# Partition sums of the modulation and gates of a decoder block: reductions with a 32x32 transpose on VectorE in the place of products with ones on TensorE

## The chip, the cores and the metric

The kernel is one program on one core of a Trainium2 chip. The metric is the device time of one execution in microseconds (us); the time of a kernel is the median of its runs. Five engines matter here: TensorE (PE in the profile, with its weight loads as PEld), VectorE (DVE), ScalarE (ACT), GpSimd (POOL) and SyncE (SP, which here only issues transfers).

## The reference: what is computed

One decoder block for 512 tokens of 1024 features in float32. Only the lines around the change are shown.

```python
cs = jax.nn.silu(c)                                   # (1, 1024)
mod = cs @ ada_w[l] + ada_b[l]                        # (1, 6 * 1024)
sh_m, sc_m, gt_m, sh_f, sc_f, gt_f = jnp.split(mod, N_MOD, axis=-1)
h = modulate(rmsnorm(x, norm_mix_g[l]), sh_m, sc_m)   # h * (1 + scale) + shift
...
merged = jax.nn.sigmoid(g_a) * y_a + jax.nn.sigmoid(g_b) * y_b
x = x + gt_m[:, None, :] * (merged @ mix_w_out[l])
h = modulate(rmsnorm(x, norm_ffn_g[l]), sh_f, sc_f)
f = (jax.nn.silu(h @ ffn_w_gate[l]) * (h @ ffn_w_up[l])) @ ffn_w_down[l]
x = x + gt_f[:, None, :] * f
return rmsnorm(x, final_norm_g)
```

The six vectors of `mod` are each a product of a 1024-vector with a 1024x1024 matrix. `sh_f` and `sc_f` (the feed-forward's modulation) and `gt_m` and `gt_f` (the two gates) are what the change touches.

## The kernel before

**The large products.** Every weight matrix is split into a high and a low part (`w_..._h` by a cast on ACT, `w_..._l` by a subtraction on DVE), and a product is three matmuls: low times high, high times low, high times high. One product of 128 output features for 512 tokens is 8 x 3 = 24 matmuls of 512 columns. Such a product is named after its output: `p_ga`, `p_gb` (merge gates), `p_ya`, `p_yb` (output projections of the two mixers), `mix`, `p_fg`, `p_fu` (feed-forward gate and up), `dn_b`, `dn_t` (blocks of the down projection). Each loop goes over pairs of 128 features: in the stage of `ga` and `ya`, an iteration is two products `p_ga` and two `p_ya`; in the next stage two `p_gb` and two `p_yb`.

**The vectors of mod.** A column of `mod` is a sum over 1024 rows of `ada_w`, laid out as 8 rows in each of 128 partitions. `ada_sum` adds the 8 rows of a partition on DVE, each scaled by its element of `cs`, into `acc_f` (512 columns: 256 of the shift and 256 of the scale) or `acc_gt_m`, `acc_gt_f` (256 columns). What is then left is the sum over the 128 partitions:

- For the modulation, `mod_vecs` has four matmuls for each of the four pairs of blocks, with 128 columns of `acc_f` as the weights and one column of ones as the moving side. The sums stand in `mod_f`, one feature in each partition, and `mod_cols` makes the columns `a_f` and `s_f` of them, which the second norm uses.
- For a gate, `gate_vec` splits each `acc` into `gh` and `gl`, multiplies both by a 128x128 tile of ones (`onesr`), so that every partition of `gp_gt_m` or `gp_gt_f` holds the sum, and adds it to `gt_m` or `gt_f`, into which the bias had been loaded, spread over all partitions. `add_gated` (for `gt_m`) and `add_gated_sum` (for `gt_f`) multiply by them.

**The order of the work.** The program is written in stages, and the framework's scheduler places each instruction in its engine's queue; every engine works its queue in order. `tick()` is called after each product, and `after(n, fn)` puts work behind the n-th tick from there: the four `summed(j)` of a gate came at ticks 1, 3, 5 and 7, each `spread(j)` one tick later. Loads of weights and of `ada_w` go through three buffers (`raw`) in the order of SP's queue. `block_sums` writes weights back to DRAM through POOL's queue (`blocks`). Early in the program, DVE works on `rotary_steps` (the angles) between the first products; the lines recorded there as L62 and L64 are those of a helper.

Of the kernel before, what the change touches and what calls it, by code (L numbers as in the profile page):

```python
# [11 lines left out]
F32 = mybir.dt.float32  # L12
F32R = mybir.dt.float32r
# [3 lines left out]
ALU = mybir.AluOpType  # L17
AX = mybir.AxisListType

P = 128  # L20
S = 512
D = 1024
H = 8
KT = D // P
# [9 lines left out]
ADA = {n: i * D for i, n in enumerate(("sh_m", "sc_m", "gt_m", "sh_f", "sc_f", "gt_f"))}  # L34
# [36 lines left out]
def block_kernel(ctx, tc, x, c, positions, ada_w, ada_b, norm_mix_g, w_in, conv_w, ret_w_out,  # L71
                 conv_w_out, mix_w_out, norm_ffn_g, ffn_w_gate, ffn_w_up, ffn_w_down,
                 final_norm_g, inv_freq, decay, out):
    nc = tc.nc
    pe, vec, act, pool, sync = (InTurn(tc, e) for e in (nc.tensor, nc.vector, nc.scalar, nc.gpsimd,
                                                        nc.sync))
    mm, transpose = pe.matmul, pe.transpose

    cp = ctx.enter_context(tc.tile_pool(name="cp", bufs=1))
# [3 lines left out]
    sp = ctx.enter_context(tc.tile_pool(name="sp", bufs=4))  # L83
    ps = ctx.enter_context(tc.tile_pool(name="ps", bufs=4, space=bass.MemoryType.PSUM))
    dp = ctx.enter_context(tc.tile_pool(name="dp", bufs=1, space=bass.MemoryType.DRAM))

    def slot(name, dt=F32, shape=None):
        return tp.tile(shape or [P, S], dt, tag="slot", name=name)

    def scr(name, dt=F32, shape=None):  # L90
        return tp.tile(shape or [P, S], dt, tag="scr", bufs=12, name=name)
# [7 lines left out]
    def aux(name, shape=None):  # L99
        return ps.tile(shape or [P, S], F32, tag="aux", bufs=2, name=name)  # L100
# [18 lines left out]
    def split_act(src, name, hi=None, lo=None, eng=None):  # L119
        hi = slot(name + "_h", F32R) if hi is None else hi  # L120
        lo = slot(name + "_l", F32R) if lo is None else lo
        act.copy(hi, src)
        (eng or vec).tensor_tensor(lo, src, hi.bitcast(F32), ALU.subtract)
        return hi, lo
# [12 lines left out]
    R_ADA, R_GM, R_GF, R_CW = 0, 48, 56, 64  # L137
# [4 lines left out]
    ident = cp.tile([P, P], F32, name="ident")  # L142
    make_identity(nc, ident)
    ones32 = cp.tile([P, P], F32, name="ones32")
# [27 lines left out]
    onesr = cp.tile([P, P], F32R, name="onesr")  # L172

    vecs = []
# [10 lines left out]
    def ada_sum(pieces, n, name, a=None, k0=0):  # L185

        first = a is None
        if first:
            a = sp.tile([P, n], F32, tag="adaacc", bufs=2, name=f"acc_{name}")
        for k, w in enumerate(pieces, k0):  # L190
            if first and k == k0:
                vec.tensor_scalar_mul(a, w, cs[:, k:k + 1])
            else:
                vec.scalar_tensor_tensor(a, w, cs[:, k:k + 1], a, ALU.mult, ALU.add)
        return a

    mod = {}
# [4 lines left out]
    ada_raw = {}  # L202
    def ada_load(f, j):


        s0 = 0 if f == "m" else 3
        cols = slice(j * P, (j + 2) * P)
        ada_raw[f, j] = pieces = []
        for k in range(0, KT, 4):
            raw = wp.tile([P, 4, 2, 2 * P], F32, tag="raw", bufs=3, name=f"ada_{f}{j}_{k}")  # L210
            for q, i in ((q, i) for q in range(0, 4, 2) for i in range(2)):
                load_raw.last = sync.dma_start(raw[:, q:q + 2, i],
                                               aw6[:, k + q:k + q + 2, s0 + i, cols])
            pieces += [raw[:, q].rearrange("p s n -> p (s n)") for q in range(4)]

    def mod_scale(f, k, col):
        g = (R_GM if f == "m" else R_GF) + k
        vec.scalar_tensor_tensor(mod["a_" + f][:, k:k + 1], col, vecs[0][:, g:g + 1],
                                 mod["b_" + f][:, k:k + 1], ALU.mult, ALU.add)

    def mod_shift(f, k, cols, n):
        r = R_ADA + ADA["sh_" + f] // P + k
        vec.tensor_tensor(mod["s_" + f][:, k:k + n], cols, vecs[0][:, r:r + n], ALU.add)

    def mod_cols(f, j, pt):

        mod_scale(f, j, pt[:, 2:3])
        mod_shift(f, j, pt[:, 0:2], 2)
        mod_scale(f, j + 1, pt[:, 3:4])

    def mod_gains(f):

        r0 = R_ADA + ADA["sc_" + f] // P
        g0 = R_GM if f == "m" else R_GF
        vec.scalar_tensor_tensor(mod["b_" + f], vecs[0][:, r0:r0 + KT], 1.0, vecs[0][:, g0:g0 + KT],
                                 ALU.add, ALU.mult)

    def mod_vecs(f, j):

        pt = aux(f"mod_{f}{j}")  # L240
        a = ada_sum(ada_raw.pop((f, j)), 4 * P, f"{f}{j}")
        for i in range(4):
            mm(pt[:, i:i + 1], lhsT=a[:, i * P:(i + 1) * P], rhs=ones32[:, 0:1],
               start=True, stop=True)
        mod_cols(f, j, pt)


    def half_ss(part, s, h, name):
# [147 lines left out]
    a = ada_sum(ada_raw["m", 0][2:6], 4 * P, "m0", None, 2)  # L396
# [155 lines left out]
    def after(n, fn):  # L552
        later.append([n, fn])
# [90 lines left out]
    def proj(src, col, Ah, Al, name, eng=None):  # L644
        raw = load_raw(src, 0, KT, col, 2 * P, "w_" + name)
        for i in range(2):
            wh, wl = split(raw[:, :, i * P:(i + 1) * P], [P, KT, P], f"w_{name}{i}", eng)
            yield i, fm_gemm(acc(f"p_{name}{i}"), wh, wl, Ah, Al)
            tick()
# [137 lines left out]
    def ret_out(p):  # L787
        raw = wp.tile([P, KT, 2 * P], F32, tag="raw", bufs=3, name=f"w_ya{p}")
        src = ret_w_out[0, :, 2 * p * P:2 * (p + 1) * P].rearrange(
            "(q h e c) n -> h e c q n", h=2, e=2, c=64)  # L790
        dst = raw.rearrange("p (q e) n -> p e q n", e=2)
        for h in range(2):
            for e in range(2):
                load_raw.last = nc.sync.dma_start(dst[64 * h:64 * h + 64, e], src[h, e])
        for i in range(2):
            wh, wl = split(raw[:, :, i * P:(i + 1) * P], [P, KT, P], f"w_ya{p}{i}")
            yield i, fm_gemm(acc(f"p_ya{p}{i}"), wh, wl, ret_in, None)
            tick()

    m_a = [None] * KT  # L800
    with tc.issue_after(hlast[-1].ins):
        mod_gains("f")
    merged = [None] * KT
    for p in range(KT // 2):
        sg = {}
        for i, pt in proj(wi, COL["ga"] + 2 * p * P, Hh, Hl, f"ga{p}"):
            sg[i] = scr(f"sga{p}{i}")
            act.activation(sg[i], pt, AF.Sigmoid)
        for i, pt in ret_out(p):
            vec.tensor_tensor(sg[i], pt, sg[i], ALU.mult)  # L810
            m_a[2 * p + i] = sg[i]
        ada_load("f", 2 * p)
        mod_vecs("f", 2 * p)
        if p == 0:
            next(block_steps)
    gate = {}

    def gate_vec(name):
        gate[name] = [misc(f"{name}_{h}") for h in range(2)]
        for h in range(2):  # L820
            with tc.issue_after(load_raw.last.ins):
                nc.sync.dma_start(
                    gate[name][h],
                    ada_b[0, ADA[name] + h * S:ADA[name] + (h + 1) * S].partition_broadcast(P))
        parts = {}

        def summed(j):
            raw = wp.tile([P, KT, 2 * P], F32, tag="raw", bufs=3, name=f"ada_{name}{j}")
            col = ADA[name] + 2 * j * P
            load_raw.last = nc.sync.dma_start(raw, aw[:, :, col:col + 2 * P])  # L830
            a = ada_sum([raw[:, k] for k in range(KT)], 2 * P, f"{name}{j}")
            gh = sp.tile([P, 2 * P], F32R, tag="gh", bufs=1, name=f"gh_{name}{j}")
            gl = sp.tile([P, 2 * P], F32R, tag="gl", bufs=1, name=f"gl_{name}{j}")
            parts[j] = split_act(a, "", gh, gl)

        def spread(j):
            gh, gl = parts.pop(j)
            pt = aux(f"gp_{name}{j}")
            mm(pt[:, 0:2 * P], lhsT=onesr, rhs=gl, start=True, stop=False)
            mm(pt[:, 0:2 * P], lhsT=onesr, rhs=gh, start=False, stop=True)  # L840
            gv = gate[name][j // 2][:, (j % 2) * 2 * P:(j % 2 + 1) * 2 * P]
            vec.tensor_tensor(gv, gv, pt[:, 0:2 * P], ALU.add)

        for j in range(4):
            after(2 * j + 1, lambda j=j: summed(j))
            after(2 * j + 2, lambda j=j: spread(j))

    for p in range(KT // 2):
        sg = {}
# [3 lines left out]
        for i, pt in proj(conv_w_out[0], 2 * p * P, conv_in, None, f"yb{p}"):  # L853
            f = 2 * p + i
# [98 lines left out]
    for i in range(2):  # L953
        wh, wl = [], []
        for k in range(0, KT, 4):
            h, l = split_act(raw[:, k:k + 4, i * P:(i + 1) * P], "",
                             slot(f"w_fg0{i}_{k}h", F32R, [P, 4, P]),
                             slot(f"w_fg0{i}_{k}l", F32R, [P, 4, P]))
# [196 lines left out]
    for h in range(2):  # L1155
# [15 lines left out]
        for t, cs in tm_gemm(ffn_w_down[0], af, f0, nf, h, groups, nf - 6, "dn", True):  # L1171
# [10 lines left out]
            r = sp.tile([P, 1], F32, tag="rr", name=f"nf_{t}_r")  # L1182
            i = 1 + cs.start // HS
            act.activation(r, ss3[t][:, i:i + 1], AF.Sqrt, scale=1.0 / D, bias=ss3[t][:, 0:1])
            vec.reciprocal(r, r)
            for i in (1, 0):
                o = scr(f"o_{t}{i}")
# [40 lines left out]
```

## Time and profile before

| | us |
|---|---|
| median of 3 runs | 947.89 |
| lowest and highest of them | 947.38, 948.22 |
| the profiled execution: its own time | 947.26 |
| its span, first to last instruction | 945.2 |
| PE busy in the span | 936.5 |
| DVE busy | 634.4 |
| ACT busy | 363.2 |
| POOL busy | 9.5 |

The span is 2.1 us shorter than the execution's time: that is what lies around the instructions. A row of the timeline has the start and the length of an instruction (or of several alike, with their count), the engine, the line, the operation, output and inputs by their names in the program, and the shapes. Matmuls overlap: each of 512 columns is shown as 0.39 us long, and the next starts about 0.23 us after it. So a matmul's price is the distance between starts, not its length.

### The profile page before, as it was taken

The numbers are of one execution on the slowest core, as the hardware profiler recorded it, in microseconds if no ns is written. First come the engines' busy times: TensorE is split into PE (matmuls) and PEld (weight loads), VectorE is DVE, ScalarE is ACT, GpSimd is POOL, SyncE is SP. The second block draws the span as 40 slices with busy tenths as digits, with TensorE's granted clock in tenths as the row PEclk, the third lists the DMA queues.
The fourth block names the chain that finished last, engine by engine and source line by source line (L and its number), as shares of the span: only waits on it lengthen the run. The fifth ranks groups of instructions, "written<-read, shape, count | busy, mean of one in ns | idle before, by whom it ended". The sixth has DMA issues, their size and how long they took to land.

```text
span 945.2 us, 11083 instructions
## 1 busy us (share of the span) xinstructions
PE 936.5 (99%) x4367; PEld 783.7 (83%) x4367; DVE 634.4 (67%) x981; ACT 363.2 (38%) x537; POOL 9.5 (1%) x26
## 2 busy tenths in 40 slices
PE   9999999999999999999999999999999999999997
PEld 8888888888888888888888888988888888888886
DVE  5989784898778755654664457657787535883346
ACT  7535333554453423222223335524433234433224
POOL 2000000000000000000000000000000000000000
PEclk9999999999999999999999999999999999999999
DMA  9943412321642447776463541455666752553102
GB/s 311 348 151 112 155 52 94 101 94 53 227 139 89 142 134 240 198 205 218 130 196 120 165 150 42 135 161 172 211 190 209 243 172 89 178 179 112 67 22 89
DMA packets 113619, 144.02 MB, mean 152 GB/s; under 512 B 4180, under 2 KB 93312, under 8 KB 112544
## 3 DMA queue, kind: packets, MB, share of 16 engines
q1 hardware_dynamic: 112048, 134.50, 44.7%
q0 software_dynamic: 1376, 8.57, 2.4%
q8 instruction: 34, 0.56, 0.3%
q10 hardware_dynamic: 144, 0.26, 0.1%
q14 instruction: 17, 0.14, 0.0%
HBM read 132.83 MB, written 10.49 MB: 152 GB/s over the span
## 4 chain that ended last, share of the span: by engine, by line
PE 98%; DVE 0%; ACT 0%; issue 0%; POOL 0%; ACTq 0%; POOLq 0%
PE p_fu L64 13%; PE p_fg L64 12%; PE p_ga L64 5%; PE p_g L64 5%; PE p_gb L64 5%; PE p_v L64 5%; PE p_yb L64 5%; PE dn_t L64 5%; PE p_ya L64 5%; PE p_q L64 5%; PE p_k L64 4%; PE p_b L64 3%; PE p_u L64 3%; PE p_c L64 3%; PE dn_b L64 3%; PE dn L64 3%
## 5 line engine op out<-in xcount | busy, mean ns | idle before, releaser
L64 PE MATMUL p_fu<-Gh,w_fu_l 128*128 128x512 f32 x160 | 62.3, 389 | 0.0
L64 PE MATMUL p_fu<-Gh,w_fu_h 128*128 128x512 f32 x160 | 62.3, 389 | 0.0
L64 PE MATMUL p_fg<-Gh,w_fg_l 128*128 128x512 f32 x160 | 62.3, 389 | 0.0
L64 PE MATMUL p_fg<-Gh,w_fg_h 128*128 128x512 f32 x160 | 62.2, 389 | 0.0
L64 PE MATMUL p_fu<-Gl,w_fu_h 128*128 128x512 f32 x160 | 62.2, 389 | 0.0
L64 PE MATMUL p_fg<-Gl,w_fg_h 128*128 128x512 f32 x160 | 62.2, 389 | 0.0
L64 DVE TENSOR_TENSOR w_fg_l<-w_fg,w_fg_h 128x1024 fp32r<-128x1024 f32 x20 | 24.4, 1222 | 36.7 <-ACT w_fg_h L64 36.7
L64 ACT CAST w_fu_h<-w_fu 128x1024 fp32r<-128x1024 f32 x20 | 21.1, 1054 | 60.5 <-PE p_fu L64 34.2
L64 ACT ACTIVATE fg<-p_fg 128x512 f32<-128x512 f32 x22 | 13.2, 598 | 73.8 <-PE p_fg L64 73.6
L64 DVE TENSOR_TENSOR fg<-p_fu,fg 128x512 f32<-128x512 f32 x22 | 15.2, 690 | 36.2 <-PE p_fu L64 36.2
L64 DVE TENSOR_TENSOR w_b_l<-w_b,w_b_h 128x1024 fp32r<-128x1024 f32 x18 | 22.0, 1221 | 19.8 <-ACT w_b_h L64 19.8
L64 PEld LDWEIGHTS p_fg<-Gh,w_fg_l 128*128 128x128 f32 x160 | 30.0, 188 | 6.2
L64 PEld LDWEIGHTS p_fg<-Gl,w_fg_h 128*128 128x128 f32 x160 | 30.0, 188 | 6.2
L64 PEld LDWEIGHTS p_fu<-Gh,w_fu_h 128*128 128x128 f32 x160 | 30.0, 188 | 6.2
L64 PEld LDWEIGHTS p_fu<-Gl,w_fu_h 128*128 128x128 f32 x160 | 30.0, 188 | 6.2
L64 PEld LDWEIGHTS p_fu<-Gh,w_fu_l 128*128 128x128 f32 x160 | 30.0, 188 | 6.2
L64 PEld LDWEIGHTS p_fg<-Gh,w_fg_h 128*128 128x128 f32 x160 | 30.0, 188 | 6.2
L64 DVE TENSOR_TENSOR w_bl<-w_bl 128x512 f32<-128x512 f32 x32 | 22.0, 689 | 7.5 <-DMA w_bl<-in_ffn_w_down_dram 7.1
L64 DVE TENSOR_TENSOR w_fu_l<-w_fu,w_fu_h 128x1024 fp32r<-128x1024 f32 x20 | 24.4, 1220 | 3.9 <-ACT w_fu_h L64 3.9
L64 ACT CAST sh<-sm 128x512 fp32r<-128x512 f32 (+3 forms) x32 | 14.7, 458 | 31.7 <-DVE sm L64 31.7
L64 DVE SCALAR_TENSOR_TENSOR acc_f<-ada_f,cs,acc_f 128x512 f32<-128x512 f32 x28 | 21.0, 750 | 8.7 <-DMA ada_f<-in_ada_w_dram 7.8
L64 ACT CAST w_b_h<-w_b 128x1024 fp32r<-128x1024 f32 x18 | 18.9, 1051 | 18.6 <-PE p_fu L64 8.0
(420 smaller groups left out, 2731.4 us busy)
## 6 DMA issues: line engine op xcount, KB each, us to landing
w_fg<-in_ffn_w_gate_dram SPq DMA_DIRECT2D x11, 1024.0 KB, 5.4
w_fu<-in_ffn_w_up_dram SPq DMA_DIRECT2D x11, 1024.0 KB, 5.4
ada_m<-in_ada_w_dram SPq DMA_DIRECT2D x32, 256.0 KB, 5.9
w_bl<-in_ffn_w_down_dram SPq DMA_DIRECT2D x16, 512.0 KB, 4.6
blocks<-w_bl POOLq DMA_DIRECT2D x8, 1024.0 KB, 4.7
ada_f<-in_ada_w_dram SPq DMA_DIRECT2D x32, 256.0 KB, 4.3
w_t<-blocks SPq DMA_DIRECT2D x8, 1024.0 KB, 5.9
w_b<-in_ffn_w_down_dram SPq DMA_DIRECT2D x6, 1024.0 KB, 5.0
```

Source lines behind the costliest of these rows:

```text
L64: self.last = op(*args, **kw)
```

## The change

`quarters`, once, early: from the identity matrix `ident`, DVE makes `quart_sum`, in which row p has a one in each column c with c mod 32 = p mod 32 (summing over the four quarters of the partitions, for each place in a quarter), and `quart_own` (which quarter a partition is in). `quarter_sums` reduces an `acc` on DVE with `apply_transpose`: each 32x32 block is transposed on the way in and summed, so that of 32 partitions and 32 columns one column of 32 sums is left, a sum for each column and quarter. One matmul with `quart_sum` then adds the four quarters.

- Modulation: `mod_part` does `ada_sum` and the reduction into `quart_f`; after all four, `mod_whole` has one matmul and five small instructions on DVE.
- Gates: `summed` does `ada_sum` and the reduction into `part`; they come at ticks 1, 3, 5 and 6. `spread` comes at tick 7: one matmul (32 x 32 out), a 32x32 transpose on DVE, the addition of the bias, and then transfers on POOL's queue: the 4 KB of the gate to DRAM (`line`), and two reads that spread a half of it over all partitions. The bias is loaded by POOL as 32x32.

```diff
-    def mod_vecs(f, j):
-        pt = aux(f"mod_{f}{j}")
-        a = ada_sum(ada_raw.pop((f, j)), 4 * P, f"{f}{j}")
-        for i in range(4):
-            mm(pt[:, i:i + 1], lhsT=a[:, i * P:(i + 1) * P], rhs=ones32[:, 0:1],
-               start=True, stop=True)
-        mod_cols(f, j, pt)
+    QP = P // 4
+    def quarters():
+        quart["sum"] = cp.tile([P, 4, QP], F32, name="quart_sum")
+        cols = sp.tile([P, QP], F32, tag="quart", bufs=1, name="quart_cols")
+        vec.tensor_reduce(cols, ident.rearrange("p (q c) -> p c q", q=4), axis=AX.X, op=ALU.add)
+        vec.tensor_copy(quart["sum"], cols.unsqueeze(1).to_broadcast([P, 4, QP]))
+        quart["own"] = cp.tile([P, 4], F32, name="quart_own")
+        vec.tensor_reduce(quart["own"], ident.rearrange("p (q c) -> p q c", q=4), axis=AX.X,
+                          op=ALU.add)
+        quart["f"] = cp.tile([P, 2 * D // QP], F32, name="quart_f")
+    def quarter_sums(o, a):
+        vec.tensor_reduce(o, a.rearrange("p (j c) -> p j c", c=QP), axis=AX.X, op=ALU.add,
+                          apply_transpose=True)
+    def mod_part(j):
+        a = ada_sum(ada_raw.pop(("f", j)), 4 * P, f"f{j}")
+        n = 4 * P // QP
+        quarter_sums(quart["f"][:, j // 2 * n:(j // 2 + 1) * n], a)
+    def mod_whole():
+        pt = aux("mod_f")[:, 0:2 * D // QP]
+        mm(pt, lhsT=quart["sum"].rearrange("p q c -> p (q c)"), rhs=quart["f"], start=True,
+           stop=True)
+        each = scr("mod_each")[:, 0:2 * D // QP].rearrange("p (n q) -> p n q", q=4)
+        vec.tensor_tensor(each, pt.rearrange("p (n q) -> p n q", q=4),
+                          quart["own"].unsqueeze(1).to_broadcast([P, 2 * KT, 4]), ALU.mult)
+        cols = sp.tile([P, KT // 2, 2, 2], F32, tag="quart", bufs=1, name="mod_cols")
+        vec.tensor_reduce(cols.rearrange("p a s b -> p (a s b)"), each, axis=AX.X, op=ALU.add)
...
@@ stages
         mod_gains("f")
+        quarters()
...
         ada_load("f", 2 * p)
-        mod_vecs("f", 2 * p)
+        mod_part(2 * p)
         if p == 0:
             next(block_steps)
+    mod_whole()
...
     def gate_vec(name):
         gate[name] = [misc(f"{name}_{h}") for h in range(2)]
-        for h in range(2):
-            with tc.issue_after(load_raw.last.ins):
-                nc.sync.dma_start(
-                    gate[name][h],
-                    ada_b[0, ADA[name] + h * S:ADA[name] + (h + 1) * S].partition_broadcast(P))
+        bias = sp.tile([QP, QP], F32, tag="gbias", bufs=1, name=f"bias_{name}")
+        nc.gpsimd.dma_start(
+            bias, ada_b[0, ADA[name]:ADA[name] + D].rearrange("(j c) -> j c", c=QP))
+        part = sp.tile([P, QP], F32, tag="gpart", bufs=1, name=f"part_{name}")
         def summed(j):
...
-            gh = sp.tile([P, 2 * P], F32R, tag="gh", bufs=1, name=f"gh_{name}{j}")
-            gl = sp.tile([P, 2 * P], F32R, tag="gl", bufs=1, name=f"gl_{name}{j}")
-            parts[j] = split_act(a, "", gh, gl)
-        def spread(j):
-            gh, gl = parts.pop(j)
-            pt = aux(f"gp_{name}{j}")
-            mm(pt[:, 0:2 * P], lhsT=onesr, rhs=gl, start=True, stop=False)
-            mm(pt[:, 0:2 * P], lhsT=onesr, rhs=gh, start=False, stop=True)
-            gv = gate[name][j // 2][:, (j % 2) * 2 * P:(j % 2 + 1) * 2 * P]
-            vec.tensor_tensor(gv, gv, pt[:, 0:2 * P], ALU.add)
-        for j in range(4):
-            after(2 * j + 1, lambda j=j: summed(j))
-            after(2 * j + 2, lambda j=j: spread(j))
+            n = 2 * P // QP
+            quarter_sums(part[:, j * n:(j + 1) * n], a)
+        def spread():
+            pt = aux(f"gp_{name}")[0:QP, 0:QP]
+            mm(pt, lhsT=quart["sum"][:, 0], rhs=part, start=True, stop=True)
+            row = sp.tile([QP, QP], F32, tag="grow", bufs=1, name=f"row_{name}")
+            vec.transpose(row, pt)
+            vec.tensor_tensor(row, row, bias, ALU.add)
+            line = dp.tile([QP, QP], F32, tag="gline", bufs=2, name=f"line_{name}")
+            nc.gpsimd.dma_start(line, row)
+            for h in range(2):
+                nc.gpsimd.dma_start(
+                    gate[name][h], line[h * QP // 2:(h + 1) * QP // 2].rearrange(
+                        "j c -> (j c)").partition_broadcast(P))
+        for j, n in enumerate((1, 3, 5, 6)):
+            after(n, lambda j=j: summed(j))
+        after(7, spread)
```

The scheduler places the new instructions, and it moves others around them. Three places matter below. The first is DVE's queue in the stage of the angles (`ang`, `ah`, `fy` are the angles' tiles). The difference of the two programs there:

```order
 L64 SCALAR_TENSOR_TENSOR b_f<-vecs 128x8
+L64 TENSOR_REDUCE quart_cols<-ident 128x32
 L62 COPY ah<-angh 128x256
+L64 COPY quart_sum<-quart_cols 128x128
 L62 TENSOR_TENSOR ah<-ang,ah 128x256
+L64 TENSOR_REDUCE quart_own<-ident 128x4
 L62 TENSOR_SCALAR fy<-ah 128x512
```

Three instructions are put in between those of the angles, and everything behind them on DVE comes later by what they cost.

The second is DVE's queue a little later, at the rotation of the first heads: `k_a`, `k_b`, `q_a`, `q_b` are its tiles, `k_l` and `q_l` the low parts of its results, and `w_g_l` is the low part of the weights of the second product `p_g`. Before:

```order
L64 TENSOR_TENSOR k_l<-k_a,k_h 128x512
L64 TENSOR_TENSOR q_b<-p_q_937,ropeS 64x512
L64 TENSOR_TENSOR w_g_l<-w_g_1013,w_g_h 128x1024
L64 TENSOR_TENSOR q_a<-q_a,q_b 128x512
L64 TENSOR_TENSOR q_a<-p_q_976,ropeC 128x512
L64 TENSOR_TENSOR q_b<-p_q_976,ropeS 64x512
L64 TENSOR_TENSOR q_l<-q_a,q_h 128x512
L64 TENSOR_TENSOR q_b<-p_q_976,ropeS 64x512
L64 TENSOR_TENSOR w_k_l<-w_k_1089,w_k_h 128x1024
L64 TENSOR_TENSOR q_a<-q_a,q_b 128x512
```

And in the changed program, at the same place of DVE's queue:

```order
L64 TENSOR_TENSOR k_l<-k_a,k_h 128x512
L64 TENSOR_TENSOR q_a<-q_a,q_b 128x512
L64 TENSOR_TENSOR q_a<-p_q_976,ropeC 128x512
L64 TENSOR_TENSOR q_b<-p_q_976,ropeS 64x512 x2
L64 TENSOR_TENSOR q_l<-q_a,q_h 128x512
L64 TENSOR_TENSOR q_a<-q_a,q_b 128x512
L64 TENSOR_TENSOR w_g_l<-w_g_1013,w_g_h 128x1024
L64 TENSOR_TENSOR q_l<-q_a,q_h 128x512
L64 TENSOR_TENSOR w_k_l<-w_k_1089,w_k_h 128x1024 x2
```

`w_g_l` has moved back past six instructions of the rotation.

The third is POOL's queue from the last of the first group of `blocks` on. The changed program:

```order
L799 DMA blocks_2305<-w_bl_3286 128x2048
L877 DMA line_gt_m<-row_gt_m 32x32
L857 DMA bias_gt_f<-in_ada_b_dram 32x32
L879 DMA gt_m_3886<-line_gt_m 128x512
L879 DMA gt_m_3887<-line_gt_m 128x512
L799 DMA blocks_2306<-w_bl_5520 128x2048
L877 DMA line_gt_f<-row_gt_f 32x32
L879 DMA gt_f_5134<-line_gt_f 128x512
L879 DMA gt_f_5135<-line_gt_f 128x512
L799 DMA blocks_2306<-w_bl_5956 128x2048
```

Before, only the three rows of `blocks` stood there; the gates' transfers are new on this queue, each pair of reads behind the write of its `line`.

More of the change, by code (lines that the diff above doesn't have):

```diff
@@ L236, in mod_gains @@
                                  ALU.add, ALU.mult)
-    def mod_vecs(f, j):
-        pt = aux(f"mod_{f}{j}")
-        a = ada_sum(ada_raw.pop((f, j)), 4 * P, f"{f}{j}")
-        for i in range(4):
-            mm(pt[:, i:i + 1], lhsT=a[:, i * P:(i + 1) * P], rhs=ones32[:, 0:1],
-               start=True, stop=True)
-        mod_cols(f, j, pt)
+    QP = P // 4
+    quart, own, mod_q = {}, {}, {}
+    def quarters():
[23 more added lines that the diff above has]
+        vec.tensor_reduce(cols.rearrange("p a s b -> p (a s b)"), each, axis=AX.X, op=ALU.add)
+        a, b, s = (mod[f"{v}_f"].rearrange("p (a b) -> p a b", b=2) for v in "abs")
+        g, r = (vecs[0][:, c:c + KT].rearrange("p (a b) -> p a b", b=2)
+                for c in (R_GF, R_ADA + ADA["sh_f"] // P))
+        vec.tensor_tensor(a, cols[:, :, 1], g, ALU.mult)
+        vec.tensor_tensor(a, a, b, ALU.add)
+        vec.tensor_tensor(s, cols[:, :, 0], r, ALU.add)
     def half_ss(part, s, h, name):
@@ L819, in gate_vec @@
         gate[name] = [misc(f"{name}_{h}") for h in range(2)]
-        for h in range(2):
-            with tc.issue_after(load_raw.last.ins):
-                nc.sync.dma_start(
-                    gate[name][h],
-                    ada_b[0, ADA[name] + h * S:ADA[name] + (h + 1) * S].partition_broadcast(P))
-        parts = {}
+        bias = sp.tile([QP, QP], F32, tag="gbias", bufs=1, name=f"bias_{name}")
+        nc.gpsimd.dma_start(
+            bias, ada_b[0, ADA[name]:ADA[name] + D].rearrange("(j c) -> j c", c=QP))
+        part = sp.tile([P, QP], F32, tag="gpart", bufs=1, name=f"part_{name}")
         def summed(j):
```

## The prediction

> **What bounds the kernel now.** I read the totals first, then the chain of work that ended last, then PE's own waits.
>
> ```profile
> span 945.2 us, 11083 instructions
> PE 936.5 (99%) x4367; PEld 783.7 (83%) x4367; DVE 634.4 (67%) x981; ACT 363.2 (38%) x537; POOL 9.5 (1%) x26
> PE 98%; DVE 0%; ACT 0%; issue 0%; POOL 0%; ACTq 0%; POOLq 0%
> ...
> PE idle L64 <- POOL ident masks.py:199: 1.5, 1, 1.5
> PE p_c L62 <- ACT Hh L62: 0.4, 1, 0.4
> PE y L64 <- ACT sh L64: 0.2, 1, 0.2
> ```
>
> PE is busy for 99% of the span, the chain is PE for 98%, and PE's waits (columns: us in total, times, longest) sum to 2.1 us in the whole program, 1.5 of them before the first matmul. So the kernel is a stream of matmuls, and an edit is worth what it takes out of the stream, less the waits that it puts in. DVE's 67% matters only where one of its results becomes the last thing that a matmul waits for.
>
> **Removed from PE: the modulation's ones-products.** The timeline of PE at the last of the four places, and the row of the tile:
>
> ```profile
> 451.51 0.39 PE L64 MATMUL p_ya<-ri_h,w_ya_h 128*128 128x512 f32 x1
> 451.73 0.95 PE L64 MATMUL mod_f<-ones,acc_f 128*128 128x1 f32 x8
> 452.54 0.48 PE L64 MATMUL p_gb<-Hh,w_gb_l 128*128 128x512 f32 x1
> 452.86 0.39 PE L64 MATMUL p_gb<-Hl,w_gb_h 128*128 128x512 f32 x1
> ...
> L64 PE MATMUL mod_f<-ones,acc_f x32: 165/250/250, 383.8 to 452.4; 128*128 128x1 f32 x32
> ```
>
> The four matmuls of one output column stand as eight records (32 in all for 16), so each is worked in two parts. A 512-column matmul is 0.227 us after the one before it. Without `mod_f` the second `p_gb` would start at 451.51 + 2 x 0.227 = 451.96; it starts at 452.86. One place costs 0.90 us, though it has one column: the eight weight loads set the pace. Four places: **3.6 us**.
>
> **Removed from PE: the gates' ones-products.** One of the eight places:
>
> ```profile
> 485.05 0.39 PE L64 MATMUL p_gb<-Hh,w_gb_h 128*128 128x512 f32 x1
> 485.27 0.28 PE L64 MATMUL gp_gt_m<-gl_gt_m,onesr 128*128 128x256 f32 x1
> ...
> 485.51 0.39 PE L64 MATMUL p_yb<-ci_h,w_yb_l 128*128 128x512 f32 x1
> ...
> 490.98 0.39 PE L64 MATMUL p_yb<-ci_h,w_yb_l 128*128 128x512 f32 x1
> ```
>
> From the first `gp_gt_m` to the next product's first matmul but one product later are 490.98 - 485.27 = 5.71 us, of which 24 x 0.227 = 5.44 are the `p_yb` between: 0.27 us a place. Two gates with four places each: 8 x 0.27 = **2.2 us**.
>
> **Added to PE.** Three matmuls: `mod_whole` (128 columns of weights, 64 moving) and a `spread` for each gate (32 of weights, 32 moving), all float32 like `mod_f`, so two records each. Two of the eight records above are a quarter of 0.90, 0.22 us; if the loss at the end of the group (452.86 - 452.54 is 0.32 in place of 0.23) is not shared out, 0.20 + 0.09 = 0.29. From below nothing is excluded but a gain: at least 0.1 for each, one record's pace. I take 0.25 for each, near `mod_f`'s row, since it is the same kind: **+0.75 us**, ends 0.3 and 0.9.
>
> [...]
>
> **Added to DVE, early.** The three instructions of `quarters` stand in the one stretch where DVE has no time to spare, and the scheduler moves `w_g_l` there. Rows: DVE's busy time in that stretch (third number after PE and PEld), the instructions around `w_g_l`, the weight load that uses it, the price of a short DVE instruction, and how soon a load follows its DVE result.
>
> ```profile
> 59.60:108.00 48.40, 48.40 (x215) 40.10 (x214) 47.78 (x91) 18.75 (x27) 0.00 (x0) 1.00 0.38 121
> ...
> 61.52 0.30 DVE L62 COPY ah<-angh 128x256 f32<-128x256 f32 x1
> ...
> 98.81 1.23 DVE L64 TENSOR_TENSOR w_g_l<-w_g,w_g_h 128x1024 fp32r<-128x1024 f32 x1
> 99.95 0.69 DVE L64 TENSOR_TENSOR q_a<-q_a,q_b 128x512 f32<-128x512 f32 x1
> 100.55 0.69 DVE L64 TENSOR_TENSOR q_a<-p_q,ropeC 128x512 f32<-128x512 f32 x1
> ...
> 103.42 1.23 DVE L64 TENSOR_TENSOR w_k_l<-w_k,w_k_h 128x1024 fp32r<-128x1024 f32 x1
> ...
> 104.25 0.19 PEld L64 LDWEIGHTS p_g<-Hh,w_g_l 128*128 128x128 f32 x1
> ...
> L64 DVE TENSOR_TENSOR sm<-st,dec 128x128 f32<-128x128 f32 x8 | 2.3, 288 | 2.5 <-PE st L64 2.4
> ...
> 227.96 0.55 DVE L64 TENSOR_TENSOR sl<-sm,sh 128x384 fp32r<-128x384 f32 x1
> ...
> 228.56 0.19 PEld L64 LDWEIGHTS y<-sl,v_h 128*128 128x128 f32 x1 [0.44 <-DVE sl L64]
> ```
>
> DVE is busy 47.78 of 48.40 us there, so what is put in is passed on. Two reductions over 128 elements at 0.29 (the row of 128x128) and a copy at 0.30 at most are 0.88 us end to end; neighbours that don't depend on each other overlap by 0.09 (99.95 + 0.69 against 100.55), five times here: I take 0.4. `w_g_l` moves past six instructions: the five from 99.95 to 103.42 in 3.47 us and a second `q_a` sum (0.60): 98.81 + 4.07 + 1.23 + 0.4 = 104.51 is its end, where it was 100.04. The load follows at once (227.96 + 0.55 = 228.51, load at 228.56), so at 104.56 where it stood at 104.25: 0.3 us late. A load stands one matmul ahead of its use, which takes up a part: **+0.2 us**, from 0 to 0.8 if nothing overlaps. Behind 108 us the added 0.4 meets idle time.
>
> [...]
>
> **Added to DVE, later, at no cost.** The reductions with a transpose: the nearest row is a reduction without one, and I bound them by it once and twice (0.69 and 1.4 us for 512 columns). Their cover, and that of the loads that move on SP's queue, with the gate of the feed-forward's rows behind:
>
> ```profile
> L64 DVE TENSOR_REDUCE v_m<-p_v 128x4 f32<-128x512 f32 x8 | 5.5, 687 | 7.8 <-PE p_v L64 7.8
> ...
> 429.40 0.74 DVE L64 SCALAR_TENSOR_TENSOR acc_f<-ada_f,cs,acc_f 128x512 f32<-128x512 f32 x1
> ...
> 478.81 0.37 SPq L108 DMA_DIRECT2D w_yb<-in_conv_w_out_dram  x1
> 482.93 0.55 SPq L830 DMA_DIRECT2D ada_gt_m<-in_ada_w_dram  x1
> ...
> 494.17 1.22 DVE L64 TENSOR_TENSOR w_yb_l<-w_yb,w_yb_h 128x1024 fp32r<-128x1024 f32 x1
> ...
> 647.52 2.57 DVE L64 SCALAR_TENSOR_TENSOR acc_gt_f<-ada_gt_f,cs,acc_gt_f 128x256 f32<-128x256 f32 x5
> ...
> 671.69 0.69 DVE L64 TENSOR_TENSOR fg<-p_fu,fg 128x512 f32<-128x512 f32 x1 [2.61 <-PE p_fu L64]
> ...
> 674.97 1.22 DVE L64 TENSOR_TENSOR w_b_l<-w_b,w_b_h 128x1024 fp32r<-128x1024 f32 x1
> ...
> 686.28 0.69 DVE L64 TENSOR_TENSOR du<-du,gt_f 128x512 f32<-128x512 f32 x1
> ...
> 688.05 1.23 DVE L64 TENSOR_TENSOR w_t_l<-w_t,w_t_h 128x1024 fp32r<-128x1024 f32 x1 [0.35 <-ACT w_t_h L64]
> ...
> 693.52 0.19 PEld L64 LDWEIGHTS dn_t<-w_t_l,s_h 128*128 128x128 f32 x1
> ...
> out_dram<-o SPq DMA_DIRECT2D x7, 256.0 KB, 2.1
> gt_f<-in_ada_b_dram SPq DMA_DIRECT2D x2, 256.0 KB, 7.3
> rows<-in_norm_mix_g_dram POOLq DMA_DIRECT2D x1, 4.0 KB, 5.5
> ```
>
> The last `acc_f` ends at 430.14 and `mod_whole`'s matmul stands where the last `mod_f` did, at 451.73: 21 us for one reduction. The last `acc_gt_f` ends at 650.09 and the gate's matmul stands behind the product that `fg` waits for, at about 671.5: 21 us again. What the DVE saves (sixteen instructions on 256 columns for the gates, twelve on one or two columns for `mod_f`, and eight casts on ACT) was beside PE's work and counts nothing. On SP's queue the last `ada_gt_m` load goes ahead of `w_yb`, and `ada_gt_f` ahead of `w_fu`; `w_yb` then gets the buffer that frees at 482.93 in place of 478.81, 4.1 us later, and has 11.2 us until DVE reads it, against 7.3 for the slowest of these landings. The four bias loads leave SP.
>
> **The gate's way by DRAM.** For `gt_m` the reader is far behind. For `gt_f` it is near: the transpose stands behind `fg`, the sum with the bias ahead of `w_b_l` (674.97), so the row is ready at about 675.2. Then two transfers in sequence on POOL, each waiting for the one before; POOL has nothing else to do but a `blocks` write that had gone out. Each lands between 2.1 us (the quickest row of 256 KB) and 5.5 for the small or 7.3 for the spread one: the gate is there between 679.4 and 688.0. It is read at 686.28, or 0.27 earlier as the `gp_gt_f` pair behind it is gone. Past that DVE waits, with `w_t_l` queued behind; `w_t_l` ends at 689.28 for a load at 693.52, so 4.2 us more are covered, until about 690.9 for the gate. The worst rows leave 2.9 us: **0**.
>
> **Sum.** -3.6 - 2.2 + 0.75 + 0.2 = -4.85, say -4.8 us: span 940.4, the profiled execution's 947.26 would be 942.5. It ran 0.63 below the median of the runs; against 947.89 the forecast is **943.1 us**. PE's stream is shorter and nothing that it waits for moves by more than its cover, so what is late next is `w_g_l`.
>
> **Rivals.**
>
> *The early stretch gives it back (in part).* If `quarters` costs not 0.4 but 2 to 3 us on the full DVE (a reduction read at long steps), `w_g_l`'s load is 1.9 to 2.9 us late, and PE waits that long: 945 to 946. For: 47.78 of 48.40 busy, and an order that has used up the spare time. Against: every short DVE row costs under 0.5 us. Chance 0.07. Beyond 3 us late the gain is within what can't be told from nothing. [...]
>
> *The gate comes late (the other side).* The transfers through DRAM replace a sum in place. If the two take over 22.8 us together, the gate is there after 698, DVE holds `w_t_l` back for 7 us, and PE waits more than the 5.0 us saved by 1.9: slower, 950 at a landing of 698, and a microsecond for each beyond. Between 691 and 698 it eats the gain. For: three serial steps with a wait each, where the nearest spread load took 7.3 us. Against: even the slowest rows give 12.8 us, and it has to be 10 more. Chance 0.04 for slower, 0.04 for a tie.
>
> *The matmuls added cost what those removed did.* If a float32 matmul of 64 columns, or one waiting for its DVE sum, costs not 0.25 but over 1 us, three cost 3 us: 945.5. Against: `mod_f`'s pace. Chance 0.03.
>
> **Chances and range.** The forecast, -5.5 to -3.8 by the ends of its terms (cheap gate matmuls and no late load; 0.9 and 0.8), 942.4 to 944.1, has 0.82. The spread of the runs is 0.5 either way. The range 941.9 to 945.6 takes in most of the early rival and of the third, and leaves out less than 2 in 10. About 0.2%, 1.9 us, is what can be told from no change here: faster by more (below 946.0) has 0.82 + 0.06 + 0.02 = 0.90, the same 0.06, slower 0.04.
>
> **What would show it.** In the trace after: no `mod_f` until one place of two records ahead of the first `p_gb`; the second matmul behind it about 0.25 us late, not 0.90; one `gp_gt_m` and one `gp_gt_f`. PE's waits still under 3 us, with at most a new one of some tenths, at `p_g` near 104.5, on DVE's `w_g_l`. DVE's `quart` instructions near 61.5 adding about 0.4 us. `du<-du,gt_f` not waiting on a transfer, or not so long that PE's `dn_t` shows a wait. The forecast is wrong if PE has a wait of over 1 us at either place, or if the starts of `p_ga` behind `p_ya` are not 0.90 us closer.

## The result, and the profile after

The changed kernel takes **942.55 us** (median of 6 runs, 942.23 to 942.80); the kernel before took 947.52 in the same rounds (6 runs, 947.38 to 948.22). The ratio is 0.9945, with a 95% interval of 0.9935 to 0.9954: faster by 5.0 us. The forecast was 943.1, from 941.9 to 945.6. The profiled execution of the changed kernel took 942.61, its span is 940.8 (945.2 before).

The totals, the chain and PE's own waits of the changed kernel:

```profile
span 940.8 us, 11007 instructions
PE 931.3 (99%) x4325; PEld 778.0 (83%) x4325; DVE 634.2 (67%) x977; ACT 359.9 (38%) x529; POOL 13.8 (1%) x34
PE 97%; DMA 1%; DVE 1%; ACT 1%; issue 0%; SPq 0%; ACTq 0%
...
PE idle L64 <- POOL ident masks.py:199: 1.5, 1, 1.5
PE tx L62 <- DVE x L62: 0.9, 1, 0.9
PE p_c L62 <- ACT Hh L62: 0.4, 1, 0.4
PE y L64 <- ACT sh L64: 0.2, 1, 0.2
```

PE has 5.2 us less busy time and 42 records less, and DVE is where it was (634.2 against 634.4). The one new wait, `tx`, is 11 us after the start, ahead of anything that the change touches; it has another size in each trace below (0 to 0.8 us), so it is scatter of the start. No wait on `w_g_l`, on a gate or on `quart_sum` stands in the list.

The place where the last `mod_f` was, on PE's timeline, and one of the two places of the gates, on PE's and then on that of its weight loads:

```profile
448.92 0.40 PE L64 MATMUL p_ya<-ri_h,w_ya_h 128*128 128x512 f32 x1
449.16 0.33 PE L64 MATMUL mod_f<-quart_f,quart_sum 128*128 128x64 f32 x2
449.30 0.48 PE L64 MATMUL p_gb<-Hh,w_gb_l 128*128 128x512 f32 x1
449.61 0.40 PE L64 MATMUL p_gb<-Hl,w_gb_h 128*128 128x512 f32 x1
...
509.04 0.39 PE L64 MATMUL p_yb<-ci_h,w_yb_h 128*128 128x512 f32 x1
509.36 0.25 PE L64 MATMUL gp_gt_m<-part_gt_m,quart_sum 128*32 128x32 f32 x2
509.54 0.50 PE L64 MATMUL p_yb<-ci_h,w_yb_l 128*128 128x512 f32 x1
509.88 0.39 PE L64 MATMUL p_yb<-ci_l,w_yb_h 128*128 128x512 f32 x1
...
508.82 0.19 PEld L64 LDWEIGHTS p_yb<-ci_h,w_yb_h 128*128 128x128 f32 x1
509.36 0.14 PEld L64 LDWEIGHTS gp_gt_m<-part_gt_m,quart_sum 128*32 128x32 f32 x2 [0.35 <-issue]
```

Without `mod_f`, the second `p_gb` would start at 448.92 + 2 x 0.227 = 449.37; it starts at 449.61: **0.24 us**, and the pair was forecast at 0.25. Without `gp_gt_m`, the second `p_yb` would start at 509.04 + 0.45 = 509.49; it starts at 509.88: **0.39 us**, above the forecast's upper end of 0.3. The place of `gt_f` costs 0.38. The loads suggest why: those of 128 columns stand one matmul ahead of their use (508.82 for the matmul of 509.04), while that of 32 columns starts only at 509.36, with its matmul and 0.32 us behind the start of the matmul ahead, and PEld was idle for 0.35 us before it. A run below tests this.

DVE early (the first four rows), `w_g_l` at its late place, and the weight load that uses it:

```profile
61.56 0.37 DVE L64 TENSOR_REDUCE quart_cols<-ident 128x32 f32<-128x128 f32 x1
...
62.05 0.22 DVE L64 COPY quart_sum<-quart_cols 128x128 f32<-128x128 f32 x1
...
62.52 0.28 DVE L64 TENSOR_REDUCE quart_own<-ident 128x4 f32<-128x128 f32 x1
62.72 0.42 DVE L62 TENSOR_SCALAR fy<-ah 128x512 f32<-128x512 f32 x1
...
103.05 1.22 DVE L64 TENSOR_TENSOR w_g_l<-w_g,w_g_h 128x1024 fp32r<-128x1024 f32 x1
...
104.33 0.19 PEld L64 LDWEIGHTS p_g<-Hh,w_g_l 128*128 128x128 f32 x1
```

`w_g_l` ends at 104.27 and its load starts at 104.33, in step with the matmuls around it: just in time, for nothing. The reduction with long steps (`quart_cols`, which adds columns 32 apart) takes 0.37 us where the one over neighbours (`quart_own`) takes 0.28. The two write 32 and 4 columns, but short sums are not dear in themselves: `mod_cols`, 16 columns of sums over four neighbours (128x64 in), took 0.21 us.

The gate of the feed-forward by DRAM: POOL's issues, DVE's reading of it, and the transfers' time from issue to landing (last column, us):

```profile
670.85 0.51 POOL L877 DMA_DIRECT2D line_gt_f<-row_gt_f  x1 [13.35 <-DVE row_gt_f L64]
672.73 1.10 POOL L879 DMA_DIRECT2D gt_f<-line_gt_f  x2 [1.37 <-DMA line_gt_f<-row_gt_f]
...
681.84 0.69 DVE L64 TENSOR_TENSOR du<-du,gt_f 128x512 f32<-128x512 f32 x1
...
gt_f<-line_gt_f POOLq DMA_DIRECT2D x2, 256.0 KB, 3.6
...
line_gt_f<-row_gt_f POOLq DMA_DIRECT2D x1, 4.0 KB, 1.6
```

The second spread transfer goes out by 673.3 (two issues from 672.73) and lands 3.6 us later, at 676.9: 4.9 us ahead of the reading. And the reductions with a transpose, on DVE (third number in ns: least, median, most):

```profile
L64 DVE TRANSPOSE_TENSOR_REDUCE quart_f<-acc_f x4: 700/711/711, 362.8 to 429.9; 128x16 f32<-128x512 f32 x4
...
L64 DVE TRANSPOSE_TENSOR_REDUCE part_gt_f<-acc_gt_f x4: 446/446/448, 604.6 to 641.8; 128x8 f32<-128x256 f32 x4
```

**By stages.** Worked out from the starts of PE's records: from the first `p_c` to the first `p_ga`, on to the first `p_gb` (the modulation), to the first `mix` (the gate `gt_m`), and to the last matmul (`gt_f`), in us. What lies ahead of `p_c` scatters by 0.7 (18.81 to 19.53 us in these traces) and is left out.

| kernel | p_c to p_ga | to p_gb | to mix | to the last | sum |
|---|---|---|---|---|---|
| before | 342.97 | 90.55 | 88.20 | 397.69 | 919.41 |
| changed | 343.02 | 87.19 | 87.58 | 397.11 | 914.90 |
| changed, again (e11) | 342.97 | 87.19 | 87.58 | 397.12 | 914.86 |
| modulation alone (e1) | 342.97 | 87.19 | 88.40 | 397.89 | 916.44 |
| gates alone (e2) | 342.93 | 90.55 | 87.54 | 397.12 | 918.13 |
| no matmul (e4) | 343.18 | 87.04 | 87.04 | 396.63 | 913.90 |
| no matmul, again (e12) | 343.04 | 87.04 | 87.04 | 396.63 | 913.74 |
| wide gate weights (e3) | 343.05 | 87.19 | 87.45 | 397.18 | 914.86 |
| quarters late (e6) | 342.92 | 87.18 | 87.58 | 397.10 | 914.79 |
| w_g_l held (e9) | 344.13 | 87.19 | 87.58 | 397.12 | 916.03 |

### The profile page after: what moved, and what is told of

It reads as the page before. It is cut to its first block, busy times and chain, and to the rows that moved or that the text cites. A ratio compares the mean times of both kernels' runs of the same rounds, so it can differ in the third digit from the quotient of the medians.

```text
span 940.8 us, 11007 instructions
## 1 busy us (share of the span) xinstructions
PE 931.3 (99%) x4325; PEld 778.0 (83%) x4325; DVE 634.2 (67%) x977; ACT 359.9 (38%) x529; POOL 13.8 (1%) x34
## 4 chain that ended last, share of the span: by engine, by line
PE 97%; DMA 1%; DVE 1%; ACT 1%; issue 0%; SPq 0%; ACTq 0%
PE p_fu L64 13%; PE p_fg L64 12%; PE p_g L64 5%; PE p_yb L64 5%; PE p_v L64 5%; PE p_gb L64 5%; PE p_ya L64 5%; PE dn_t L64 5%; PE p_ga L64 5%; PE p_q L64 5%; PE p_k L64 4%; PE p_u L64 3%; PE p_b L64 3%; PE p_c L64 3%; PE dn_b L64 3%; PE dn L64 3%
```

## The experiments

**One half at a time.** The modulation alone keeps `gate_vec` as it was before:

```diff
-        bias = sp.tile([QP, QP], F32, tag="gbias", bufs=1, name=f"bias_{name}")
 ...
-        after(7, spread)
+        for j in range(4):
+            after(2 * j + 1, lambda j=j: summed(j))
+            after(2 * j + 2, lambda j=j: spread(j))
```

> Only the modulation's half of the change; the gates are summed as before. Theory (the kernel is a stream of matmuls, and an edit is worth what it takes out of the stream): 4 places x 0.90 us less, one matmul of about 0.24 us more: -3.4 us against the kernel before, 944.1 where that is at 947.5 (ratio 0.9965). Rival 'the early stretch gives it back': the three instructions of quarters are here too, so the gain would be under 3 us, with a wait of PE at p_g. Rival 'the gain is mostly the gates' (their eight stops of DVE, ACT and PE): under 2 us here.

Measured: 944.15 (5 runs) against 947.61 before (15 runs), ratio 0.9962 (0.995 to 0.9975): -3.5 us, as the theory has it. The stage of the modulation lost 90.55 - 87.19 = 3.36 us; the early stretch has no wait at `p_g`. (The two gate stages are 0.2 us longer each than before, where no difference was due. It is spread over all of them: in the stage of `gt_m` the mean distance of two matmuls of 512 columns is 227.5 ns here and 227.0 before; why is open.)

The gates alone keep `mod_vecs`:

```diff
-        mod_part(2 * p)
+        mod_vecs("f", 2 * p)
 ...
-    mod_whole()
```

> Only the gates' half; the modulation keeps its sixteen one-column matmuls. Theory: 8 x 0.27 us less, two matmuls of 32 columns more. With the 0.39 us that each shows in the trace of the changed kernel: -1.4 us against the kernel before (ratio 0.9985); with the 0.25 of the prediction -1.7. Rival 'the gate comes late': a wait of DVE on gt_f, and less gain or none. If the two halves don't add up to the whole (-4.4 by the profiles), something else has moved.

Measured: 945.88 (11 runs) against the same 947.61, ratio 0.9981 (0.9972 to 0.9989): -1.7 us, an interval that holds both sizes. The trace leans to the 1.4: the two gate stages lost 0.66 and 0.57, 1.2 us together. The halves add up: 3.5 + 1.7 = 5.2 for 5.0 by the runs, and 3.36 + 1.2 = 4.6 for 4.5 by the stages. The other two stages are where they were.

**Why a gate's matmul costs 0.39 us.**

```diff
-            pt = aux(f"gp_{name}")[0:QP, 0:QP]
-            mm(pt, lhsT=quart["sum"][:, 0], rhs=part, start=True, stop=True)
+            nq = 4 if name == "gt_m" else 2
+            pt = aux(f"gp_{name}")[0:nq * QP, 0:QP]
+            mm(pt, lhsT=quart["sum"][:, 0:nq].rearrange("p q c -> p (q c)"), rhs=part, start=True,
+               stop=True)
 ...
-            vec.transpose(row, pt)
+            vec.transpose(row, pt[0:QP])
```

> The changed kernel with more columns of weights in the gates' matmuls: 128 (all of quart_sum) for gp_gt_m, 64 for gp_gt_f, instead of 32; only the first 32 rows of the result are used. Theory: a load of 32 columns isn't pulled ahead of the running matmul and so stands bare in the stream; with 128 columns the place costs what mod_f's does, 0.24 us instead of 0.39, and 64 columns tell where it turns. Rival: the 0.39 us come from the moving side (32 columns) or from the wait for part, and stay with 128 columns too.

Measured, on PE's timeline and on that of its loads, for the 128 columns of `gp_gt_m` and then the 64 of `gp_gt_f`:

```profile
509.08 0.40 PE L64 MATMUL p_yb<-ci_h,w_yb_h 128*128 128x512 f32 x1
...
509.77 0.40 PE L64 MATMUL p_yb<-ci_l,w_yb_h 128*128 128x512 f32 x1
...
509.08 0.42 PEld L64 LDWEIGHTS gp_gt_m<-part_gt_m,quart_sum 128*128 128x128 f32 x2
...
666.61 0.39 PE L64 MATMUL p_fu<-Gh,w_fu_h 128*128 128x512 f32 x1
...
667.49 0.39 PE L64 MATMUL p_fu<-Gl,w_fu_h 128*128 128x512 f32 x1
...
666.92 0.19 PEld L64 LDWEIGHTS gp_gt_f<-part_gt_f,quart_sum 128*64 128x64 f32 x2 [0.35 <-issue]
```

With 128 columns the load starts with the matmul ahead (509.08), and the place costs 509.77 - 509.08 - 0.45 = **0.24 us**. With 64 it starts 0.31 us behind the start of the matmul ahead, and the place costs 667.49 - 666.61 - 0.45 = 0.43, which is 0.05 more than with 32 columns there: its two loads take 0.19 us together, where those of 32 columns take 0.14. The theory holds, and the rival falls: the moving side and the wait for `part` were the same. Why a narrow load starts later, the traces do not show. The whole kernel shows little of it (one run, 942.58; the stage of `gt_m` is 0.13 shorter, that of `gt_f` 0.06 longer).

**Without the three matmuls.** The last sum over the four quarters is done on DVE, and `quarters` is gone (for the gates; the modulation alike, with four copies back to the partitions):

```diff
-            mm(pt, lhsT=quart["sum"][:, 0], rhs=part, start=True, stop=True)
+            for q in range(4):
+                vec.tensor_copy(side[:, q], part[q * QP:(q + 1) * QP])
+            vec.tensor_reduce(tot, side.rearrange("p q c -> p c q"), axis=AX.X, op=ALU.add)
 ...
-            vec.transpose(row, pt)
+            vec.transpose(row, tot)
```

> The whole change, and the last sum over the four quarters of the partitions taken off TensorE too: four copies that bring the quarters side by side into 32 partitions, and one reduction, on DVE; for the modulation four copies back. quarters is gone. Theory: the three added matmuls cost 0.24 + 2 x 0.39 = 1.0 us of the stream, so 1.0 us less than the changed kernel: 941.5 where that is at 942.5, -5.8 to -6.0 against the kernel before (ratio 0.9938). Rival 'they stand where PE would have waited anyway': no difference to the changed kernel. Rival 'small copies cost DVE more than is free there': a new wait of PE, slower than the changed kernel.

Measured: 941.71 (5 runs) against 947.61, ratio 0.9936 (0.9923 to 0.995). It was run again beside the changed kernel, on the same chip:

> The changed kernel itself, on the same chip and in the same rounds as the version without matmuls: 942.5, -5.0 us against the kernel before.

> The version without the three matmuls again, beside the changed kernel: 1.0 us under it by the stream (0.24 + 2 x 0.39), 941.5. Rival: the first measurement of 941.7 was the scatter of a call, and the two agree within 0.3 us.

Measured: the changed kernel 942.38 (942.24 to 942.67, ratio 0.9943, 0.993 to 0.9956), this one 941.68 (941.44 to 941.70, ratio 0.9934, 0.992 to 0.9948), against 947.67 before. So 0.7 us under the changed kernel, 0.3 less than expected, with runs that don't overlap. By the stages the three are worth 0.15 + 0.54 + 0.49 = 1.2 us, 0.2 more than expected. In the profiled pair 0.1 of it was lost again in the early stretch and 0.5 ahead of `p_c` (first `p_c` at 19.29 here, 18.81 in the changed kernel; 19.05 and 19.09 in the pair measured first), which scatters; whether the runs' missing 0.3 us are that is open. This is the quickest version of all. Its totals:

```profile
span 939.9 us, 11007 instructions
PE 931.1 (99%) x4319; PEld 778.3 (83%) x4319; DVE 638.6 (68%) x991; ACT 360.4 (38%) x529; POOL 13.8 (1%) x34
```

DVE has 4.4 us more and PE's waits are none more.

**Is the early stretch a price?** First `quarters` taken out of it:

```diff
     with tc.issue_after(hlast[-1].ins):
         mod_gains("f")
-        quarters()
 ...
+        if p == 0:
+            with tc.issue_after(vec.last.ins):
+                quarters()
```

> The changed kernel with the three instructions of quarters put behind the stretch in which DVE is full, at the first place of the modulation (about 300 us later). Theory after the trace: w_g_l was late by no more than its slack, so this gains 0 to 0.1 us over the changed kernel. The prediction's term: 0.2 us. Rival 'the early stretch gives back': 0.5 us or more, seen as an earlier p_g.

Measured: 942.8 (5 runs), ratio 0.9947 (0.9934 to 0.9959): no gain, and 0.05 to 0.1 us in the stage. Then more put in:

```diff
-        vec.tensor_reduce(cols, ident.rearrange("p (q c) -> p c q", q=4), axis=AX.X, op=ALU.add)
+        for _ in range(6):
+            vec.tensor_reduce(cols, ident.rearrange("p (q c) -> p c q", q=4), axis=AX.X, op=ALU.add)
```

> The changed kernel with the reduction that makes quart_cols done six times: 5 x 0.28 to 0.37 us = 1.4 to 1.9 us more on DVE in the full stretch. Theory: the slack there is small (w_g_l was ready 0.06 us before its load), so PE waits for most of it, +1.0 to 1.9 us at p_q, p_g or p_k by 108 us. Rival: the order bends round it (w_g_l goes ahead of work that can wait), and nothing is seen: within 0.2 us of the changed kernel.

Measured: 942.42 (4 runs), ratio 0.9946 (0.9929 to 0.9963): nothing, so my theory of a full stretch without slack fell. Two things bent. The order changed: `w_g_l` went ahead of the `q_a` work and ended at 100.73 in place of 104.27. And the five added reductions of 0.37 us each moved the first `w_q_l` only 0.7 us against the first `c<-p_u` at the head of the stretch (26.59 us behind it, 25.88 in the changed kernel): put between the steps of a chain, where each needs the one ahead, they fill time that was lost there. How much, the kernel before shows in the same chain: `fy<-fy` starts 0.46 us after the `fy<-ah` that it needs (62.31, 62.77), and the `fr<-ah` that does not need it only 0.35 us later (63.12), for steps of 0.43 us. So I put nine in and held `w_g_l` where the changed kernel has it:

```diff
+        for _ in range(9):
+            vec.tensor_reduce(cols, ident.rearrange("p (q c) -> p c q", q=4), axis=AX.X, op=ALU.add)
 ...
+            with tc.issue_after(roped[3].ins):
+                vec.tensor_tensor(lo, src, hi.bitcast(F32), ALU.subtract)
```

> The changed kernel with the reduction that makes quart_cols done nine times, and the second w_g_l held behind the second q_a sum, where the changed kernel has it. With six times and no hold w_g_l went ahead of the q_a work and PE waited for nothing, and five more reductions moved DVE by 0.7 us only (they fill the gaps of a chain). So eight more are 1.1 us here, 2.2 if they fill nothing. Theory (the slack of w_g_l at its late place is 0.06 us, give or take 0.4 by where a run's DVE stands against PE): PE waits 0.5 to 1.5 us at p_g near 104.5. Rival (the stretch has slack enough for it wherever w_g_l stands): no wait, and the time stays at 942.5.

Measured: 943.69 (one run), and PE's waits:

```profile
PE p_g L64 <- DVE w_g_l L64: 0.3, 1, 0.3
PE p_k L64 <- DVE w_k_l L64: 0.3, 1, 0.3
```

The stretch is 1.1 us longer than in the changed kernel (344.13 against 343.02), half of it at each of the two places (`p_k` near 82.5 us, `p_g` near 104.9). So the wait that the prediction named can be had, and the slack at that place is as small as the trace says; but it takes work that the order can't step round. One run shows it.

**Is DVE's work later hidden?**

```diff
-        vec.tensor_reduce(o, a.rearrange("p (j c) -> p j c", c=QP), axis=AX.X, op=ALU.add,
-                          apply_transpose=True)
+        for _ in range(4):
+            vec.tensor_reduce(o, a.rearrange("p (j c) -> p j c", c=QP), axis=AX.X, op=ALU.add,
+                              apply_transpose=True)
```

> The changed kernel with each of the eight reductions with a transpose done four times (12 x 0.71 + 12 x 0.45 = 14 us more of DVE). Theory: they have some 21 us of cover before the matmul that reads them, so the time stays within 0.2 us of the changed kernel. Rival: DVE's 67% hides less than that, and weights come late: +0.5 us or more.

Measured: 942.51 (4 runs), ratio 0.9946 (0.9931 to 0.9961). The reductions are twelve and not eight (four of the modulation, four for each gate), so the expected 14 us are too few: DVE's busy time grew by 16.9 us (651.1 against 634.2), and the time did not.

**When does the gate come late?** The row of `gt_f` goes through more rows in DRAM, each copied from the one ahead on POOL's queue:

```diff
             nc.gpsimd.dma_start(line, row)
+            for i in range(HOPS if name == "gt_f" else 0):
+                hop = dp.tile([QP, QP], F32, tag="hop", bufs=HOPS, name=f"hop_{i}")
+                nc.gpsimd.dma_start(hop, line)
+                line = hop
```

With three:

> As the run with eight more rows, but three: at 2 to 3 us each the gate lands at 683 to 686 instead of 677. Theory: it is read at 681.8 in the changed kernel, so DVE waits or does the rest first, and PE has cover until 690: within 0.3 us of the changed kernel. Rival: any landing behind 681.8 stops PE, as the weights for its next products are queued behind the reading: +1 us or more.

Measured: 942.22 (one run). DVE waited 2.47 us for the gate, and PE for nothing:

```profile
683.83 0.69 DVE L64 TENSOR_TENSOR du<-du,gt_f 128x512 f32<-128x512 f32 x1 [2.47 <-DMA gt_f<-hop]
```

With eight:

> The changed kernel with the feed-forward's gate sent through eight more rows in DRAM, one behind the other, before it is spread. A step took 1.4 to 1.9 us from issue to issue (the transfer of 4 KB 1.6), so the gate lands 12 to 16 us later, at 689 to 693 instead of 677. Theory of the cover: DVE waits for it at du (about 7 to 11 us), and PE only from about 686.5 + 4.2 (times of the changed kernel): a wait of PE at dn_t of 0 to 3 us. Rival: the cover is less than worked out, and PE waits 5 us or more; or more than that, and PE doesn't wait at all.

Measured: 950.46 (one run, before 947.55), 7.9 us more than the changed kernel. DVE's timeline, PE's wait, and the busy times of PE, PEld, DVE, ACT and POOL with PE's granted clock (PEclk, the first number behind them) in the windows around it:

```profile
694.26 1.23 DVE L64 TENSOR_TENSOR w_b_l<-w_b,w_b_h 128x1024 fp32r<-128x1024 f32 x1 [1.75 <-ACT w_b_h L64]
700.78 1.29 DVE L64 TENSOR_TENSOR du<-du,gt_f 128x512 f32<-128x512 f32 x2 [5.30 <-DMA gt_f<-hop]
...
708.60 1.21 DVE L64 TENSOR_TENSOR w_b_l<-w_b,w_b_h 128x1024 fp32r<-128x1024 f32 x1
...
PE dn_b L64 <- DVE w_b_l L64: 6.3, 1, 6.3
...
700.00:703.00 3.00, 3.00 (x15) 2.49 (x14) 2.22 (x4) 1.11 (x2) 0.00 (x0) 1.00 0.18 71
703.00:709.86 6.86, 0.56 (x3) 0.14 (x1) 6.86 (x12) 0.97 (x1) 0.00 (x0) 0.76 0.00 0
709.86:713.00 3.14, 3.14 (x7) 2.49 (x8) 2.82 (x3) 0.00 (x0) 0.00 (x0) 0.50 0.61 181
...
hop<-hop POOLq DMA_DIRECT2D x7, 4.0 KB, 3.0
```

The theory's 0 to 3 us missed, its rival's 5 us or more came. Three things show. The copies took 2.1 to 2.2 us from issue to issue at first and 2.6 to 4.8 later (last row: the median of seven of them from issue to landing), so the gate came at 700.8 and not by 693. What had gathered behind `du` then ran for 7.8 us ahead of the next `w_b_l` (700.78 to 708.60). And behind its 6.3 us of waiting, PE ran at a granted clock of 0.50 for some 3.5 us: some eight matmuls 0.43 us apart in place of 0.23, 1.7 us more. The mechanism of the prediction's second rival is shown: a late gate does stop PE, through the weights queued behind it. Its size isn't: with 950 at a landing of 698 and a microsecond for each beyond, a gate at 700.8 (705.2 in the time of before) would have made 957. The order had bent here too: the first reading of the gate stands behind the `w_b_l` of 694.26, five splits of weights later than in the changed kernel, where it is at 681.84. The point from which it does lies between a gate at 683.8 (nothing) and one at 700.8 (8 us), against 676.9 in the changed kernel; where between was not tried, and it goes by the order that DVE's queue then has.

## Why the prediction was right

The mechanism is as forecast: PE's stream got shorter by what was taken out of it, and PE waits for nothing new. Term by term, against the traces:

| term | forecast | measured | from |
|---|---|---|---|
| modulation's products out | -3.6 | -3.6 | stage -3.36, with 0.24 for `mod_f` |
| gates' products out | -2.2 | -2.0 | the two gate stages, -1.20, with 2 x 0.39 put in; 0.24 for each of eight by the starts |
| three matmuls in | +0.75 | +1.02 | 0.24 + 2 x 0.39 |
| late `w_g_l` | +0.2 | 0 to 0.1 | first stage, changed against before and against e6 |
| sum | -4.85 | -4.5 | 919.41 - 914.90 |

- **The step that was mis-sized** is "I take 0.25 for each, near `mod_f`'s row, since it is the same kind". It was right for `mod_whole` (0.24), and wrong for the gates' two (0.39 and 0.38, with an upper end of 0.3): a load of 32 columns isn't the same kind, as the run with wide weights shows. The third rival, over 1 us for each, fell. The gates' old products were a little too dear in the forecast: its 0.27 a place is what was left of a stretch of 24 other matmuls, and the starts at the place itself (485.27 to 485.51) give 0.24.
- **The narrow loads themselves** are short: the two of a gate start 28 ns apart, and their records are 106 to 109 ns long where one of 128 columns has 188, 80 ns more. The place is dearer all the same, 0.39 us against 0.24: its first load starts 0.32 us behind the start of the matmul ahead, where one of 128 columns starts with it (e3, both at 509.08).
- **The early stretch.** `quarters` moved DVE by 0.3 us (25.88 against 25.57 from the first `c<-p_u` to the first `w_q_l`), forecast 0.4, and `w_g_l` ended at 104.27, forecast 104.51. The 0.2 us were too many: there was no wait. The reduction read at long steps, which the first rival names, took 0.37 us against 0.28 for the one over neighbours with the same 128x128 in: the difference of 0.09 was too small to matter here.
- **The first rival** (the stretch gives it back) had its point at 2 to 3 us of `quarters`. With six reductions the records sum to over 2 us, but DVE came only 1.0 us later than before (26.59 against 25.57), and nothing was given back; with nine and the order held DVE came 1.5 us later (27.02), and 1.1 us came back. A delay of 2 us was not reached.
- **The gate by DRAM** was to land between 679.4 and 688.0 in the time of before, which is 675 to 684 in the changed kernel (4.4 us earlier there): 676.9, near the quick end. The cover behind the reading was to last until 690.9 (686.28 and 4.2 are 690.5), and the run with three copies shows 2.5 us of it.
- **The reductions** cost what the lower bound said (0.71 for 0.69 us), hidden as forecast.
- **The time itself.** 942.55 is 0.55 below the forecast, although the terms took out 0.35 less than forecast, so the number owes something to luck. 0.4 us are the reference: the forecast started from 947.89, and before ran at 947.5 to 947.7 in every later set. The rest is that the medians fell by 5.0 us and not 4.8, though the stages of the profiles fell by only 4.5. About half of the 0.5 between lies outside the span: what lies around the instructions is 2.0 to 2.2 us in the runs of before and 1.8 to 1.9 in those of the changed kernel, some 0.2 us that no term held; why is open. The other half is the profile of before: its span of 945.2 is 0.3 below the 945.5 that its later runs have in the middle. Which part of the program scatters so, with one profile of before, is open.
- **The range.** Its dear end was added up wrong: -3.6 - 2.2 + 0.9 + 0.8 is -4.1, not -3.8. The part of the range that it bounds is 942.4 to 943.8, and the measured time lies in it either way.

## What to carry to other kernels

When one engine is busy for 99% of the span, price an edit by the distances between the starts on that engine's timeline, ahead of and behind the place, and price each added instruction by its own shape: a matmul with narrow weights cost more here than one with full weights (0.39 us with 32 columns, 0.24 with 128). A full engine is not yet a price, either: work put between the steps of a chain costs less than its length (0.14 us for 0.37 here), and the scheduler's order can step round it; what makes it a price is one result that is just in time and can't be moved. The last cheap matmuls of a reduction over partitions can leave PE altogether, by copies between partitions on an engine with room (0.7 us less by the runs here, for 4.4 us more on DVE).

## What was not expected of the hardware

- A weight load of 128 columns ahead of a small matmul started together with the matmul in front; loads of 32 and 64 columns started 0.32 and 0.31 us behind its start. The narrow loads are the shorter ones (106 to 109 ns one of 32 columns, 0.19 us both of 64 together, against 188 ns one of 128), and their places the dearer ones: 0.39 and 0.43 us against 0.24.
- Reductions with a transpose cost about the same as a plain one: 0.71 us for 128x512, where the plain one of 128x512 took 0.69.
- A copy of 32x32 between partitions on DVE took 0.17 us, and each reduction of 0.37 us that was put between chained steps moved what follows by about 0.14 (0.71 for five).
- After a gap of 6.3 us PE's granted clock was 0.50 for some 3.5 us, so that the stall cost 8 us. It is one gap in one run.
